# Gated products of a conv feed-forward and rotary steps, moved from GpSimd to VectorE

## The chip, the cores and the metric

The kernel runs on one core of a Trainium2 chip. The metric is the device time of one execution in microseconds (us); lower is better. Engine names are those of the profile: PE is TensorE (PEld its weight loads), DVE is VectorE, ACT is ScalarE, POOL is GpSimd, SP the engine that issues most transfers.

## What is computed

Two transformer-like blocks of two layers each, on 256 tokens of width 1024, in float32. A layer of the first block mixes tokens (a Fourier branch and a retention branch whose queries and keys are rotated), then runs a feed-forward with a convolution over three neighbouring tokens and a gate. A layer of the second block has pooling, a spatial gate and an attention whose latent queries and keys are rotated, then a squared-ReLU feed-forward. The parts that the change touches:

```python
def rotary(t):                    # block 1: queries and keys of the retention
    t1, t2 = t[..., :half], t[..., half:]
    return concatenate([t1 * cos - t2 * sin, t1 * sin + t2 * cos], axis=-1)

def conv_ffn(h, w_up, conv_w, conv_b, w_down):          # block 1
    u = h @ w_up                                        # 1024 -> 2 * 2816
    u = sum(pad(u)[:, i:i + S] * conv_w[i] for i in range(3)) + conv_b
    a, b = split(u, 2, axis=-1)
    return (gelu(a) * b) @ w_down

def apply_rope(x, cos, sin):                            # block 2
    x1, x2 = x[..., 0::2], x[..., 1::2]
    return stack([x1 * c - x2 * s, x1 * s + x2 * c], axis=-1)
```

## The kernel before

Activations lie feature-major, 128 features by 256 tokens to a tile (512 tokens in layer 0 of the second block, which carries a context beside the latent). Every product with weights is done in three matmuls: both sides are split into a rounded part and a remainder (hi and lo), and hi.hi, lo.hi and hi.lo are summed (`mm3`, lines 174 to 176).

Weights come as a stream of 540 units of 128x1024, eight 128x128 blocks each (`Stream`). For every unit SP loads `wraw`, ACT rounds it to `whi` (line 85) and DVE subtracts to get `wlo` (line 87); PE needs `wlo` for every third matmul. Beside that DVE works off modulation vectors, each a dot product over a 128x1024 tile (line 262, `mraw` or `junk`), paced by unit numbers (`RATES1`).

The feed-forward of block 1 runs over m = 0 to 21 in each of two layers. A step m takes two products with `ffn_up` (16 blocks, two units, 48 matmuls). Of each product ACT makes `z` (line 824) and DVE adds the two neighbouring tokens to it (lines 825 and 826). Then ACT makes `ga`, the Gelu of the first `z` (line 829); POOL multiplies it with the second `z` into `gb` (line 834); and `split` makes `fh` on ACT (line 179) and `fl` on DVE (line 180) of it, the input of `ffn_down`.

In block 1 `rotary` (lines 629 to 638) makes each of two halves with two products on DVE (`ra`, `rb`, lines 633 and 634), a sum or difference on POOL (`ro`, line 636) and a `split`: 16 sums in a layer. In block 2 `roped` (lines 1019 to 1026) makes a product and a shuffle on DVE (lines 1022 and 1023), a product and a sum on POOL (lines 1024 and 1025), and a split of the result: eight times in a layer, for keys and queries of four head pairs.

The order of instructions on each engine is set when the program is built: a scheduler places them, engine by engine, from what each depends on and its own estimates. Each engine then works through its list in that order, and an instruction that waits holds up all behind it.

Of the kernel before, what the change touches and what calls it, by code (L numbers as in the profile page):

```python
# [11 lines left out]
ALU = mybir.AluOpType  # L12
# [117 lines left out]
def build(ctx, tc, a, out):  # L130
    nc = tc.nc
# [20 lines left out]
    def tt(tag, name, shape, dt=F32):  # L152
        tag = cur["alias"].get(tag, tag)
        return cur["tp"].tile(list(shape), dt, name=name, tag=tag, bufs=cur["bufs"][tag])
# [23 lines left out]
    def split(src, hi, lo):  # L178
        nc.scalar.copy(hi, src)  # L179
        nc.vector.tensor_sub(lo, src, hi.bitcast(F32))  # L180
# [35 lines left out]
    def col(name, i, n=1):  # L216
        o = COLS[name] + i
        return cols[:, o:o + n]
# [85 lines left out]
    def fm(reqs, rhs, fresh=False, at=None):  # L304

        p = ps_mm.tile([128, 512], F32, name="mm")
        n = rhs[0][0].shape[-1]
        late = []
        for i, (r, (xh, xl)) in enumerate(zip(reqs, rhs)):
            wh, wl = st.take(*r) if isinstance(r[0], str) else r  # L310
            if at and i in at:
                at[i]()
            if fresh:
                nc.tensor.matmul(p[:, :n], wh, xh, start=(i == 0), stop=False)
                nc.tensor.matmul(p[:, :n], wl, xh, start=False, stop=False)
                late.append((wh, xl))
            else:
                mm3(p[:, :n], wh, wl, xh, xl, i == 0, i == len(reqs) - 1)
        for i, (wh, xl) in enumerate(late):
            nc.tensor.matmul(p[:, :n], wh, xl, start=False, stop=(i == len(late) - 1))  # L320
        return p[:, :n]
# [214 lines left out]
    with ExitStack() as c1:  # L536
# [78 lines left out]
        cos, sin = rope[:, 0, :], rope[:, 1, :]  # L615
# [4 lines left out]
        for l in range(2):  # L620
# [7 lines left out]
            def rotary(c0, dst, ps=None):  # L628
                p1, p2 = ps or (fm(win(c0), rhs), fm(win(c0 + 128), rhs))
                for j, (ca, cb, op) in enumerate(((cos, sin, ALU.subtract), (sin, cos, ALU.add))):  # L630
                    ta = tt("r", "ra", (128, 256))
                    tb = tt("r", "rb", (128, 256))
                    nc.vector.tensor_mul(ta, p1, ca)
                    nc.vector.tensor_mul(tb, p2, cb)
                    o = tt("ro", "ro", (128, 256))
                    nc.gpsimd.tensor_tensor(out=o, in0=ta, in1=tb, op=op)
                    hi, lo = dst(j)
                    split(o, hi, lo)

            if l:  # L640
                pace["rate"] = 0
                y.shift(need(0, l, 0)[:, 0, :])
                keys = y.run([win(2 * D), win(2 * D + 128)], dst)
                kv0 = tt("kv", "kv", (128, 4, 2, 256), F32R)
                rotary(None, lambda j: (kv0[:, 0, j, :], kv0[:, 1, j, :]), keys)
# [170 lines left out]
            for m in range(M1):  # L816
                pace["rate"] = RATES1[l][4] if m else 0
                z = []
                for ab in range(2):
                    i = ab * M1 + m  # L820
                    p = first.pop(0) if first else fm(up(i), rhs2, fresh=m == 1)
                    w = lambda t: col("conv_w", (l * 3 + t) * 44 + i)
                    zz = tt("r", "z", (128, 256))
                    nc.scalar.activation(zz, p, AF.Identity, scale=w(1), bias=col("conv_b", l * 44 + i))
                    nc.vector.scalar_tensor_tensor(out=zz[:, 1:], in0=p[:, :-1], scalar=w(0), in1=zz[:, 1:], op0=ALU.mult, op1=ALU.add)  # L825
                    nc.vector.scalar_tensor_tensor(out=zz[:, :-1], in0=p[:, 1:], scalar=w(2), in1=zz[:, :-1], op0=ALU.mult, op1=ALU.add)  # L826
                    z.append(zz)
                ga = tt("ro", "ga", (128, 256))
                nc.scalar.activation(ga, z[0], AF.Gelu)
                if m % 8 == 0:  # L830
                    tg = ("kv", "A", "B")[m // 8]
                    fh, fl = tt(tg, "fh", S8, F32R), tt(tg, "fl", S8, F32R)
                o = tt("go", "gb", (128, 256))
                nc.gpsimd.tensor_tensor(out=o, in0=ga, in1=z[1], op=ALU.mult)  # L834
                split(o, fh[:, m % 8, :], fl[:, m % 8, :])
                hid.append((fh[:, m % 8, :], fl[:, m % 8, :]))
            g2 = need(0, l, 5)[:, 0, :]
# [31 lines left out]
    for l in range(2):  # L869
        with ExitStack() as c2:  # L870
# [16 lines left out]
            cos, sin = rope[:, 0, :], rope[:, 1, :]  # L887
# [54 lines left out]
            def gate(i, m):  # L942
                pg = fm(gate_w(l, i, m), rhs)
                th = tt("gt", "gt", (128, N))
                nc.scalar.activation(th, pg, AF.Tanh, scale=0.5)
                return th
# [15 lines left out]
            for j in range(2):  # L962
# [12 lines left out]
                for hf, s in ((0, s2), (1, s4)):  # L975
                    r = slice(64 * hf, 64 * hf + 64)
                    nc.vector.tensor_tensor(out=pd[r], in0=s[r, :, 8:264],
                                            in1=icnt[r, j, :].unsqueeze(1).broadcast_to((64, nseg, 256)), op=ALU.mult)
# [39 lines left out]
            def roped(p):  # L1018
                t1 = tt("r", "ra", (128, 256))
                t2 = tt("r", "rb", (128, 256))  # L1020
                o = tt("ro", "ro", (128, 256))
                nc.vector.tensor_mul(t1, p, cos)
                nc.vector.stream_shuffle(t2, p, swap)
                nc.gpsimd.tensor_tensor(out=t2, in0=t2, in1=sin, op=ALU.mult)  # L1024
                nc.gpsimd.tensor_tensor(out=o, in0=t1, in1=t2, op=ALU.add)
                return o

            def scaled_split(src, hi, lo):
# [152 lines left out]
            for m in range(KT):  # L1181
                t0, t1 = (early.pop(0) if early else gate(i, m) for i in range(2))
                branch("w_pool_out_2", m, por, t0, at(acc, m))
                o = tt("go", "go", (128, N))
# [5 lines left out]
            for m in range(KT):  # L1190
                th = gate(2, m)
                o = tt("go", "go", (128, N))
# [123 lines left out]
            if not both:  # L1316
                bc = to_rows(rsqrt_cols(sq_sums(tiles(x))))
                for k in range(KT):
                    o = tt("nu" if k < 5 else "r", "fin", (128, T))
# [95 lines left out]
def make(inputs):  # L1415
    import concourse.bacc as bacc

    arrays, A = _layout(inputs)
    nc = bacc.Bacc("TRN2", target_bir_lowering=False, num_devices=1, dynamic_dma_scratch_size=1024)
    aps = {k: nc.dram_tensor("in_" + k, v.shape, mybir.dt.from_np(v.dtype), kind="ExternalInput").ap() for k, v in arrays.items()}  # L1420
    aps["ws"] = nc.dram_tensor("in_ws", (N_UNITS, 128, 1024), F32, kind="ExternalInput").ap()
    out = nc.dram_tensor("out", (KT, 128, T), F32, kind="ExternalOutput").ap()
    with tile.TileContext(nc) as tc, ExitStack() as ctx:
        req = build(ctx, tc, aps, out)
    ins = {"in_" + k: v for k, v in arrays.items()}
    ins["in_ws"] = _pack(req, A)
    return nc, ins
# [11 lines left out]
```

## Time and profile before

| | us |
|---|---|
| median of three runs | 2169.05 (2163.69 to 2169.51) |
| the profiled execution's own time | 2171.02 |
| its span, first to last instruction | 2169.2 |
| PE busy | 2089.8 |
| DVE busy | 1681.2 |
| ACT busy | 1008.6 |
| POOL busy | 291.5 |

Busy time is the time in which an engine has at least one instruction under way; instructions of one engine overlap by some tens of nanoseconds, so that the sum of their lengths is more. Matmuls of PE overlap much more: one of 256 columns has a length of some 0.28 us, and the next starts long before it ends. What lies between span and own time is outside of the first and last instruction.

### The profile page before, as it was taken

To read this page: it belongs to the slowest core of one execution; us is meant where nothing else is said; L and a number is where in the kernel's file an instruction comes from. 1 tells how busy PE (TensorE), PEld (TensorE's weight loads), DVE (VectorE), ACT (ScalarE), POOL (GpSimd) and SP (SyncE) were. 2 spreads that over 40 slices of the span, in tenths; PEclk is the share of its full clock that TensorE was granted. 3 is DMA by queue.
4 is the path that set the end of the run, shared out by engine and by line. 5 is a ranking of instruction groups with operands and counts; after the bars stand their busy time and mean duration, and the time that the engine had idled before them with its cause. 6 is when DMAs were issued, how large, how long until landed. Compare 5 with 4: busy or idle time off the path is not lost.

```text
span 2169.2 us, 36942 instructions
## 1 busy us (share of the span) xinstructions
PE 2089.8 (96%) x14492; PEld 1923.8 (89%) x14492; DVE 1681.2 (78%) x2849; ACT 1008.6 (46%) x1670; POOL 291.5 (13%) x342
## 2 busy tenths in 40 slices
PE   7999999999999999999999999999999989999998
PEld 6999999999999998898778888888888887899998
DVE  3778888887789888897878677788787577768665
ACT  3544466545445565554553233523233454556444
POOL 0002022222012022241110001200001112101000
PEclk9999999999999999999999999999999999999999
DMA  7576756685777655663334444355554243355553
GB/s 287 190 241 218 259 189 214 223 313 193 240 272 248 219 183 196 216 223 128 110 121 146 170 162 144 117 184 177 184 183 146 88 156 97 127 185 166 185 185 118
DMA packets 112350, 401.32 MB, mean 185 GB/s; under 512 B 12592, under 2 KB 14512, under 8 KB 110896
## 3 DMA queue, kind: packets, MB, share of 16 engines
q1 hardware_dynamic: 106272, 387.82, 52.4%
q10 hardware_dynamic: 5904, 11.14, 1.6%
q8 instruction: 114, 1.87, 0.4%
q14 instruction: 60, 0.49, 0.1%
HBM read 397.87 MB, written 1.05 MB: 184 GB/s over the span
## 4 chain that ended last, share of the span: by engine, by line
PE 80%; DVE 9%; POOL 4%; issue 3%; ACT 3%; DMA 1%; POOLq 0%; ACTq 0%; SPq 0%; DVEq 0%
PE mm L175 21%; PE mm L176 21%; PE mm L174 21%; DVE wlo L87 3%; PE mm L349 2%; PE mm L344 2%; PE mm L348 2%; POOL gb L834 2%; ACT whi L85 1%; DVE z L825 1%; DVE z L826 1%; PE sc L1055 1%; PE at L1095 1%; DVE mraw L262 1%; POOL rb L1024 1%
## 5 line engine op out<-in xcount | busy, mean ns | idle before, releaser
L85 ACT CAST whi<-wraw 128x1024 fp32r<-128x1024 f32 x540 | 564.5, 1047 | 701.2 <-PE mm L175 507.9
L87 DVE TENSOR_TENSOR wlo<-wraw,whi 128x1024 fp32r<-128x1024 f32 x540 | 667.6, 1238 | 169.0 <-ACT whi L85 166.2
L176 PE MATMUL mm<-hh,wlo 128*128 128x256 f32 (+1 forms) x2112 | 659.7, 313 | 12.1 <-DVE wlo L87 12.0
L174 PE MATMUL mm<-hh,whi 128*128 128x256 f32 (+1 forms) x2112 | 660.6, 313 | 3.4 <-ACT whi L85 2.4
L175 PE MATMUL mm<-hl,whi 128*128 128x256 f32 (+1 forms) x2112 | 657.8, 311 | 0.0
L176 PEld LDWEIGHTS mm<-hh,wlo 128*128 128x128 f32 x2112 | 401.6, 190 | 38.7 <-DVE wlo L87 15.1
L174 PEld LDWEIGHTS mm<-hh,whi 128*128 128x128 f32 x2112 | 402.0, 190 | 28.7 <-ACT whi L85 3.2
L175 PEld LDWEIGHTS mm<-hl,whi 128*128 128x128 f32 x2112 | 401.9, 190 | 22.9
L176 PE MATMUL mm<-fh,wlo 128*128 128x256 f32 (+1 forms) x880 | 275.4, 313 | 3.5 <-DVE wlo L87 3.4
L174 PE MATMUL mm<-fh,whi 128*128 128x256 f32 (+1 forms) x880 | 275.4, 313 | 1.6 <-ACT fh L179 1.6
L262 DVE CUSTOM_DVE_ANT_0 mraw<-mraw,cvec,cols 128x1024 f32<-128x1024 f32 x176 | 229.5, 1304 | 0.0
L176 PEld LDWEIGHTS mm<-fh,wlo 128*128 128x128 f32 x880 | 166.3, 189 | 14.8 <-DVE wlo L87 4.3
L174 PEld LDWEIGHTS mm<-fh,whi 128*128 128x128 f32 x880 | 166.3, 189 | 12.8 <-ACT fh L179 2.0
L175 PE MATMUL mm<-fh,whi 128*128 128x256 f32 (+1 forms) x528 | 176.2, 334 | 0.0
L349 PE MATMUL mm<-wlo,hh 128*128 128x256 f32 x496 | 140.5, 284 | 3.1 <-DVE wlo L87 3.1
L344 PE MATMUL mm<-whi,hh 128*128 128x256 f32 x496 | 141.2, 286 | 0.9 <-ACT hh L441 0.9
L348 PE MATMUL mm<-whi,hl 128*128 128x256 f32 x480 | 136.3, 284 | 0.0
L395 POOL TENSOR_TENSOR acc<-acc,sq 128x256 f32<-128x256 f32 x52 | 57.1, 1101 | 511.3 <-ACT sq L393 495.2
L262 DVE CUSTOM_DVE_ANT_0 junk<-mraw,cvec,cols 128x1024 f32<-128x1024 f32 x96 | 124.7, 1299 | 0.0
L175 PEld LDWEIGHTS mm<-fh,whi 128*128 128x128 f32 x528 | 99.7, 189 | 11.5 <-DVE fh L180 0.8
L175 PE MATMUL mm<-fl,whi 128*128 128x256 f32 x352 | 99.3, 282 | 0.1
L349 PEld LDWEIGHTS mm<-wlo,hh 128*128 128x128 f32 x496 | 94.6, 191 | 3.8 <-DVE wlo L87 3.3
(320 smaller groups left out, 3590.3 us busy)
## 6 DMA issues: line engine op xcount, KB each, us to landing
wraw<-in_ws SPq DMA_DIRECT2D x540, 512.0 KB, 3.3
mraw<-in_mw SPq DMA_DIRECT2D x176, 512.0 KB, 4.3
mraw<-in_mw SPq DMA_DIRECT2D x8, 1024.0 KB, 9.0
bias<-in_na_bias ACTq DMA_DIRECT2D x16, 256.0 KB, 2.8
dm<-in_dmask ACTq DMA_DIRECT2D x8, 256.0 KB, 3.9
cvec<-in_cvec SPq DMA_DIRECT2D x3, 512.0 KB, 5.3
x<-in_x SPq DMA_DIRECT2D x1, 1024.0 KB, 5.0
cx<-in_ctx ACTq DMA_DIRECT2D x1, 1024.0 KB, 7.6
```

The source lines that it names most:

```text
L85: self.nc.scalar.copy(hi, raw)
L87: self.nc.vector.tensor_sub(lo, raw, hi.bitcast(F32))
L174: nc.tensor.matmul(o, lh, rh, start=start, stop=False)
L175: nc.tensor.matmul(o, lh, rl, start=False, stop=False)
L176: nc.tensor.matmul(o, ll, rh, start=False, stop=stop)
L262: nc.vector.tensor_tensor_reduce(out=junk if b and not v else raw, in0=raw, in1=cvec[2 * b if v else b], scale=1.0, scalar=col("b_mod_2" i ...
L344: nc.tensor.matmul(o, xh, wh, start=(k == 0 and j % 2 == 0), stop=False)
L348: nc.tensor.matmul(o, xl, wh, start=False, stop=False)
L349: nc.tensor.matmul(o, xh, wl, start=False, stop=last and not fresh)
L395: (nc.gpsimd if k in SQ_POOL else nc.vector).tensor_tensor(out=acc, in0=acc, in1=sq, op=ALU.add)
L825: nc.vector.scalar_tensor_tensor(out=zz[:, 1:], in0=p[:, :-1], scalar=w(0), in1=zz[:, 1:], op0=ALU.mult, op1=ALU.add)
L834: nc.gpsimd.tensor_tensor(out=o, in0=ga, in1=z[1], op=ALU.mult)
```

## The change

Four instructions of the source move from `nc.gpsimd` to `nc.vector`, with the same operands: `gb`, the `ro` of block 1, and both steps of `roped`. In numbers that is 44 + 32 + 16 + 16 = 108 instructions of 128x256. Loads, tiles and buffers stay.

```diff
--- before.py
+++ after.py
@@ -633,7 +633,7 @@
                     nc.vector.tensor_mul(ta, p1, ca)
                     nc.vector.tensor_mul(tb, p2, cb)
                     o = tt("ro", "ro", (128, 256))
-                    nc.gpsimd.tensor_tensor(out=o, in0=ta, in1=tb, op=op)
+                    nc.vector.tensor_tensor(out=o, in0=ta, in1=tb, op=op)
                     hi, lo = dst(j)
                     split(o, hi, lo)
 
@@ -831,7 +831,7 @@
                     tg = ("kv", "A", "B")[m // 8]
                     fh, fl = tt(tg, "fh", S8, F32R), tt(tg, "fl", S8, F32R)
                 o = tt("go", "gb", (128, 256))
-                nc.gpsimd.tensor_tensor(out=o, in0=ga, in1=z[1], op=ALU.mult)
+                nc.vector.tensor_mul(o, ga, z[1])
                 split(o, fh[:, m % 8, :], fl[:, m % 8, :])
                 hid.append((fh[:, m % 8, :], fl[:, m % 8, :]))
             g2 = need(0, l, 5)[:, 0, :]
@@ -1021,8 +1021,8 @@
                 o = tt("ro", "ro", (128, 256))
                 nc.vector.tensor_mul(t1, p, cos)
                 nc.vector.stream_shuffle(t2, p, swap)
-                nc.gpsimd.tensor_tensor(out=t2, in0=t2, in1=sin, op=ALU.mult)
-                nc.gpsimd.tensor_tensor(out=o, in0=t1, in1=t2, op=ALU.add)
+                nc.vector.tensor_mul(t2, t2, sin)
+                nc.vector.tensor_add(o, t1, t2)
                 return o
 
             def scaled_split(src, hi, lo):
```

The scheduler places the moved instructions among DVE's others, and shifts others with them. Two places show it.

DVE, layer 1 of the feed-forward, around the split of one step (before; numbers in the names tell tiles apart, `mod101` is a modulation vector):

```order
L826 SCALAR_TENSOR_TENSOR z_10343<-mm_10310,cols_108,z_10343 128x255
L262 ISA mraw_10317,mod101_122<-mraw_10317,cvec_9204,cols_108 128x1024
L262 ISA mod101_122 128x1
L180 TENSOR_TENSOR fl_9913<-gb_10349,fh_9912 128x256
L825 SCALAR_TENSOR_TENSOR z_10385<-mm_10353,cols_108,z_10385 128x255
L87 TENSOR_TENSOR wlo_10435<-wraw_10432,whi_10434 128x1024
L826 SCALAR_TENSOR_TENSOR z_10385<-mm_10353,cols_108,z_10385 128x255
L825 SCALAR_TENSOR_TENSOR z_10421<-mm_10389,cols_108,z_10421 128x255
L87 TENSOR_TENSOR wlo_10470<-wraw_10467,whi_10469 128x1024
L826 SCALAR_TENSOR_TENSOR z_10421<-mm_10389,cols_108,z_10421 128x255
L87 TENSOR_TENSOR wlo_10513<-wraw_10510,whi_10512 128x1024
L180 TENSOR_TENSOR fl_9913<-gb_10427,fh_9912 128x256
```

The same place with the change:

```order
L826 SCALAR_TENSOR_TENSOR z_10343<-mm_10310,cols_108,z_10343 128x255
L87 TENSOR_TENSOR wlo_10393<-wraw_10390,whi_10392 128x1024
L834 TENSOR_TENSOR gb_10349<-ga_10347,z_10343 128x256
L825 SCALAR_TENSOR_TENSOR z_10385<-mm_10353,cols_108,z_10385 128x255
L262 ISA mraw_10317,mod101_122<-mraw_10317,cvec_9204,cols_108 128x1024
L262 ISA mod101_122 128x1
L180 TENSOR_TENSOR fl_9913<-gb_10349,fh_9912 128x256
L826 SCALAR_TENSOR_TENSOR z_10385<-mm_10353,cols_108,z_10385 128x255
L825 SCALAR_TENSOR_TENSOR z_10421<-mm_10389,cols_108,z_10421 128x255
L87 TENSOR_TENSOR wlo_10435<-wraw_10432,whi_10434 128x1024
L826 SCALAR_TENSOR_TENSOR z_10421<-mm_10389,cols_108,z_10421 128x255
L87 TENSOR_TENSOR wlo_10470<-wraw_10467,whi_10469 128x1024
```

Before, only `mraw` stood between the second pass over `z` and `fl`; now `wlo`, `gb`, the next step's first pass (line 825) and `mraw` stand there, with `gb` behind `wlo`.

DVE, block 2 layer 0, latent queries of head pair 1 (before; `P` of the attention is transposed and split into `pt`):

```order
L1022 TENSOR_TENSOR ra<-mm,rope_12374 128x256
L1023 STREAM_SHUFFLE rb<-mm 128x256
L87 TENSOR_TENSOR wlo<-wraw,whi 128x1024
L1030 SCALAR_TENSOR_TENSOR qq<-ro,qq 128x256
L1030 SCALAR_TENSOR_TENSOR qq<-mm,qq 128x256
L180 TENSOR_TENSOR pt<-at,pt 128x4x128 x2
```

The same place with the change:

```order
L1022 TENSOR_TENSOR ra<-mm,rope_12374 128x256
L1023 STREAM_SHUFFLE rb<-mm 128x256
L87 TENSOR_TENSOR wlo<-wraw,whi 128x1024
L1024 TENSOR_TENSOR rb<-rb,rope_12374 128x256
L1030 SCALAR_TENSOR_TENSOR qq<-mm,qq 128x256
L1025 TENSOR_TENSOR ro<-ra,rb 128x256
L180 TENSOR_TENSOR pt<-at,pt 128x4x128
L1030 SCALAR_TENSOR_TENSOR qq<-ro,qq 128x256
L180 TENSOR_TENSOR pt<-at,pt 128x4x128
```

Both steps of `roped` stand behind `wlo`, and the first half of `pt` now stands ahead of the rotated queries' remainder `qq<-ro`, which came before both halves.

## Rows read from the trace of the kernel before

**Rows 1.** The page: totals of the span, and chain that ended last, by engine.

```profile
PE 2089.8 (96%) x14492; PEld 1923.8 (89%) x14492; DVE 1681.2 (78%) x2849; ACT 1008.6 (46%) x1670; POOL 291.5 (13%) x342
...
PE 80%; DVE 9%; POOL 4%; issue 3%; ACT 3%; DMA 1%; POOLq 0%; ACTq 0%; SPq 0%; DVEq 0%
```

**Rows 2.** Windows: length, busy us (instructions) of PE, PEld, DVE, ACT, POOL; clock; DMA.

```profile
795.00:910.00 115.00, 107.15 (x884) 105.35 (x883) 96.06 (x161) 66.02 (x109) 27.46 (x18) 1.00 0.64 211
354.80:440.50 85.70, 83.47 (x693) 82.54 (x692) 69.72 (x111) 50.32 (x84) 21.92 (x15) 1.00 0.64 221
540.00:690.00 150.00, 149.65 (x1258) 149.24 (x1256) 129.03 (x213) 70.56 (x107) 22.50 (x28) 1.00 0.72 246
...
1040.00:1130.00 90.00, 84.39 (x437) 65.73 (x436) 74.26 (x204) 46.62 (x109) 17.80 (x16) 0.96 0.33 112
1090.00:1100.00 10.00, 7.88 (x49) 6.53 (x49) 6.66 (x18) 4.30 (x12) 2.50 (x2) 0.87 0.29 97
```

**Rows 3.** Timeline of POOL, `gb` of both layers, with idle time before each.

```profile
354.80 1.68 POOL L834 TENSOR_TENSOR gb<-ga,z 128x256 f32<-128x256 f32 x1 [4.03 <-DVE z L826]
...
440.48 1.55 POOL L834 TENSOR_TENSOR gb<-ga,z 128x256 f32<-128x256 f32 x1 [5.11 <-DVE z L826]
...
795.86 0.74 POOL L834 TENSOR_TENSOR gb<-ga,z 128x256 f32<-128x256 f32 x1 [6.57 <-DVE z L826]
...
912.09 1.66 POOL L834 TENSOR_TENSOR gb<-ga,z 128x256 f32<-128x256 f32 x1 [4.97 <-DVE z L826]
```

**Rows 4.** Timeline of one step of layer 1: start, length, engine, idle before.

```profile
846.45 0.48 DVE L826 SCALAR_TENSOR_TENSOR z<-mm,cols,z 128x255 f32<-128x255 f32 x1
...
847.10 1.61 POOL L834 TENSOR_TENSOR gb<-ga,z 128x256 f32<-128x256 f32 x1 [5.11 <-DVE z L826]
...
848.75 0.41 ACT L179 CAST fh<-gb 128x256 fp32r<-128x256 f32 x1 [1.82 <-POOL gb L834]
...
849.19 0.43 DVE L180 TENSOR_TENSOR fl<-gb,fh 128x256 fp32r<-128x256 f32 x1 [1.06 <-ACT fh L179]
849.53 0.48 DVE L825 SCALAR_TENSOR_TENSOR z<-mm,cols,z 128x255 f32<-128x255 f32 x1
...
855.65 0.43 DVE L180 TENSOR_TENSOR fl<-gb,fh 128x256 fp32r<-128x256 f32 x1 [1.07 <-ACT fh L179]
```

**Rows 5.** Waits of 795 to 910 us: who waited for whom, us, times, longest.

```profile
ACT fh L179 <- POOL gb L834: 36.1, 17, 3.0
DVE fl L180 <- ACT fh L179: 18.1, 17, 1.1
...
PE mm L176 <- DVE wlo L87: 7.5, 8, 1.5
```

**Rows 6.** POOL by line and form, whole span: busy us, mean ns, idle before.

```profile
L834 POOL TENSOR_TENSOR gb<-ga,z 128x256 f32<-128x256 f32 x44 | 62.7, 1424 | 204.3 <-DVE z L826 183.8 <-ACT whi L85 10.9 <-ACT z L824 5.5
...
L636 POOL TENSOR_TENSOR ro<-ra,rb 128x256 f32<-128x256 f32 x32 | 32.8, 1041 | 226.8 <-DVE rb L634 180.6 <-ACT whi L85 46.3
```

**Rows 7.** DVE by line and form, whole span, columns as before.

```profile
L180 DVE TENSOR_TENSOR ql<-ro,qh 128x256 fp32r<-128x256 f32 x16 | 10.1, 628 | 1.7 <-ACT qh L179 1.5
...
L796 DVE TENSOR_TENSOR go<-go,gf 128x256 f32<-128x256 f32 x16 | 6.8, 423 | 0.4
```

**Rows 8.** Timeline of the latent queries of head pair 1, block 2 layer 0.

```profile
1092.08 1.22 DVE L87 TENSOR_TENSOR wlo<-wraw,whi 128x1024 fp32r<-128x1024 f32 x1
...
1093.97 0.73 POOL L1025 TENSOR_TENSOR ro<-ra,rb 128x256 f32<-128x256 f32 x1
...
1095.19 0.42 DVE L1030 SCALAR_TENSOR_TENSOR qq<-ro,qq 128x256 fp32r<-128x256 f32 x1 [1.89 <-ACT qq L1029]
...
1095.87 1.28 DVE L180 TENSOR_TENSOR pt<-at,pt 128x512 fp32r<-128x512 f32 x2
1096.60 3.08 PE L1095 MATMUL at<-pt,vv 128*128 128x256 f32 x16 [2.12 <-DVE pt L180]
1099.48 0.63 PE L174 MATMUL mm<-hh,whi 128*128 128x512 f32 x1
```

## The prediction

> **What bounds the kernel now.** The page's totals come first: PE is busy 96% of the span and DVE 78%, POOL only 13% [rows 1]. PE is the engine to fill, and what can be won is the time in which it lacks work. Its busy share hides a part of that, since matmul lengths overlap, so I count matmuls per time instead. In a stretch in which PE is busy 149.65 of 150 us, 1258 matmuls, nearly all of 256 columns, take 150 us: 0.119 us each [rows 2]. A step of the feed-forward, 48 matmuls, therefore needs 48 x 0.119 = 5.72 us of PE.
>
> The page's chain then says where to look: POOL has 4% of what ended last, though it is nearly idle [rows 1]. The starts of `gb`, one to a step, give the real pace of the feed-forward. In layer 1, 18 steps take 912.09 - 795.86 = 116.2 us, 6.46 us each; in layer 0, 14 steps take 440.48 - 354.80 = 85.7 us, 6.12 us each [rows 3]. Against 5.72 us PE loses 0.74 us a step in layer 1 and 0.40 us in layer 0.
>
> The windows over these steps tell who sets that pace. In layer 1 DVE is busy 96.06 of 115 us and PE's matmuls thin out; ACT has 66.02, POOL 27.46 [rows 2]. DVE is thus busy 96.06 / 115 x 6.46 = 5.39 us a step and idle for 1.07. The waits say what it is idle for: of its some 19 idle us, 18.1 lie ahead of `fl`, which waits for `fh` on ACT, and ACT waits 36.1 us for `gb` on POOL; PE in turn waits for `wlo`, DVE's work [rows 5]. One step of the timeline shows the loop: DVE ends `z`, POOL takes 1.61 us for `gb`, ACT starts `fh` at 848.75, and DVE, idle for 1.06 us, starts `fl` at 849.19; the next `fl` is at 855.65 and has waited 1.07 us [rows 4]. So DVE is the bound of layer 1, and a sixth of its time there is a wait for POOL. In layer 0 it is busy 69.72 of 85.7 us [rows 2], 4.98 us a step.
>
> **The change, part by part.**
>
> *Gated products.* 44 instructions of 1424 ns leave POOL [rows 6]. On DVE the same kind, two inputs in SBUF and 128x256, takes 423 ns [rows 7]; what it adds to the list may be less, for the instruction behind `fl` started 849.53 - 849.19 = 0.34 us after it though `fl` is 0.43 long [rows 4]. I take 0.42. `gb` no longer waits for another engine but for `ga`, which ACT finishes earlier, and DVE always has a `wlo`, a dot product or a pass over `z` between `gb` and `fl`, so that ACT's 0.41 us for `fh` [rows 4] is covered. The 1.07 us of waiting is replaced by 0.42 us of work. Behind the wait stood the next `wlo`, and behind that PE.
>
> Layer 1: a step then costs DVE 5.39 + 0.42 = 5.81 us, a little over PE's 5.72. If no idle time is left, 18 steps gain 18 x (6.46 - 5.81) = 11.7 us. I keep 0.09 us a step for waits that turn up next, the likeliest being the first pass over `z`, which waits for ACT and through it for PE: **-10 us**. The best end, with 0.34 for `gb`, is 18 x (6.46 - 5.73) = 13; the worst, all idle time kept and the work on top, is 18 x 0.42 = 7.6 us lost.
>
> Layer 0: DVE would need 4.98 + 0.42 = 5.40 us, less than PE's 5.72, so PE becomes the bound and 14 x 0.40 = 5.6 us are to be had. The dot products come at some steps and not at others, and where one comes DVE is over 5.72 for that step; I take **-4.5 us**. The ends are -5.6 and 14 x 0.42 = +5.9.
>
> *Rotary of block 1.* 32 sums of 1041 ns leave POOL [rows 6] and bring DVE 32 x 0.42 = 13.4 us. In the stretch from 540 to 690 us, in which layer 1 rotates heads, PE is busy 149.65 of 150 and DVE is idle for 21 of 150 [rows 2]: nothing to win, and room for the 5 us that fall there. **0 us.** What hides it is that idle time and the units loaded ahead; without this cover the price is at most the 13.4. DVE also gets something back: `ql`, the remainder after these sums, takes 628 ns where its shape takes 423 [rows 7], 16 x 0.2 = 3.3 us. I count neither and keep -1 and +2 as ends.
>
> *Rotary of block 2.* Two instructions for each of eight results in a layer move, 16 x 0.35 = 5.6 us of DVE a layer at the spacing seen above. DVE is busy 74.26 of 90 us in the first of the two attentions, and PE only 84.39 of 90 [rows 2]. The one clear place is the latent queries of head pair 1: POOL's second step starts at 1093.97, `qq<-ro` on DVE starts at 1095.19 after 1.89 us of idle time, `pt` is behind it, and PE stands 2.12 us until `pt`; its matmuls of 512 columns are then 0.63 us long and the granted clock of these 10 us is 0.87, so a part runs at 1.2 GHz and not at 2.4 [rows 8, 2]. In the new order `wlo` (1092.08 to 1093.30) is still followed by three instructions of some 0.35 us and then the first half of `pt`, which starts near 1094.4 rather than 1095.87: 1.5 us for PE, and I add 0.5 for the clock: **-2 us**. At the other places `wlo` or a softmax step now stands ahead of the rotation, and I expect no net effect. Ends: -5, most of the 5.6 us that PE is not busy in that stretch, and +5.6, all of one layer's added work on the path.
>
> *Queues.* No transfer moves but one modulation load, which changes places with a weight load on SP: nothing.
>
> *Sum.* -10 - 4.5 + 0 - 2 = -16.5 us. The profiled execution, 2171.0 us with what lies around its span, becomes 2154.5. It stands 2.0 us above the median of the runs, so I forecast 2169.05 - 16.5 = **2152.5 us**.
>
> So DVE gains by taking work on, though at 84% of the stretch it is the most occupied of DVE, ACT and POOL [rows 2]: its idle sixth is made by the slow engine. The Trainium skill (Perfetto Trace Analysis, Optimizing Scalar/DVE Operations) says that work may be worth moving off a saturated DVE, even to GpSimd, though the port that the two share may spoil it; by this rule the change goes the wrong way, and the time would be that of the second rival.
>
> **The rivals.**
>
> *The wait only changes its name.* `fh` stands in ACT's list between `whi` and `z`, each of which can wait for PE. If ACT comes to `fh` late in every step, DVE keeps half of its idle time: 0.53 left + 0.42 new against 1.06 is a gain of 0.11 us a step, 32 steps, some 3.5 us: 2165.5. For it: ACT is busy 66.02 of 115 us with an order of its own. Against: ACT itself sat idle 36.1 us for `gb` [rows 5], so it has been early, not late.
>
> *DVE is simply too full.* Nothing of the idle time goes, because `fl` waits for something other than POOL, and DVE's list is 0.42 us longer in each step: 18 x 0.42 + 14 x 0.42 = 13.4 us, 2182.5. It decides from 6.46 - 5.81 = 0.65 us of idle time left per step in layer 1 on; below that the change still gains. For it: DVE's own sum, 5.81, is above PE's 5.72. Against: the wait is seen to follow POOL's end, 848.71 to 848.75 to 849.19, in step after step [rows 4, 5].
>
> That the change does less than it says is ruled out by the order of DVE's list, in which the moved instructions stand.
>
> **How the numbers follow.** Forecast 0.77, its own range 2145.5 (-13 - 5.6 - 5) to 2162.5 (a third of the idle time left in both layers, nothing in attention); first rival 0.14; second rival 0.09. The range that leaves out no more than 2 in 10 is 2146 to 2165: the forecast and the near side of the first rival. About 0.3%, 6.5 us, is what a measurement of this kernel can tell from no change, so faster means below 2162.5 and slower above 2175.6. Faster: 0.77 from the forecast, and 0.02 of the first rival, less 0.01 at the forecast's edge: 0.78. Same: the rest of the first rival and 0.01 of the others, 0.14. Slower: 0.08 of the second rival.
>
> **What would show it.** In layer 1 of the feed-forward `gb` starts should be 5.8 us apart, in layer 0 5.7; the wait of `fl` for `fh` should be gone; DVE should be busy some 97% of the steps of layer 1, and PE's wait for `wlo` there, 7.5 us [rows 5], a fraction. POOL's share of the chain should fall to about 1%. PE should stay full from 540 to 690 us. If `fl` still waits half a microsecond in each step, the first rival is right; if `gb` starts are over 6.5 us apart in layer 1, the second; if the feed-forward gains 14 us and the total does not, the attention or the rotation of block 1 has taken it.

## The result and the profile after

The changed kernel takes 2133.86 us (median of four runs, 2132.19 to 2134.51), the kernel before 2168.99 us in the same comparison: a ratio of 0.9839, 95% interval 0.9827 to 0.9851. The gain is 35 us, twice the 16.5 that was forecast, and the time lies below the range given. The profiled execution took 2132.19 us, its span 2130.4.

The page after, totals and chain, answers to [rows 1]:

```profile
PE 2077.2 (97%) x14492; PEld 1916.9 (90%) x14492; DVE 1696.6 (80%) x2957; ACT 1013.5 (48%) x1670; POOL 158.8 (7%) x234
...
PE 89%; DVE 5%; ACT 2%; issue 1%; POOL 1%; DMA 1%; ACTq 0%; POOLq 0%; SPq 0%; DVEq 0%
```

DVE has 108 instructions more and only 15.4 us more of busy time. POOL's share of the chain falls from 4% to 1%, DVE's from 9% to 5%, and PE's rises from 80% to 89%.

Windows of the changed kernel over the stretches of [rows 2] (length, then busy us and instructions of PE, PEld, DVE, ACT, POOL; granted clock; DMA): layer 1 and layer 0 of the feed-forward, the head rotations of block 1, and the attentions of block 2, layer 0 and layer 1.

```profile
790.00:905.00 115.00, 115.00 (x964) 114.55 (x962) 112.46 (x191) 73.40 (x117) 0.00 (x0) 1.00 0.70 236
348.00:434.00 86.00, 86.00 (x725) 86.00 (x724) 79.86 (x133) 54.50 (x89) 0.00 (x0) 1.00 0.70 234
530.00:680.00 150.00, 149.87 (x1260) 149.54 (x1259) 130.15 (x230) 71.45 (x106) 6.38 (x14) 1.00 0.73 250
...
1010.00:1130.00 120.00, 119.55 (x636) 94.25 (x635) 108.39 (x286) 62.89 (x139) 0.55 (x1) 1.00 0.37 128
1750.00:1850.00 100.00, 99.61 (x713) 89.47 (x713) 82.36 (x214) 53.06 (x102) 3.91 (x12) 1.00 0.36 118
```

In layer 1 of the feed-forward PE is busy all of the 115 us, with 964 matmuls where there were 884, and DVE 112.46 us. In both attentions PE is busy over 99%. The next rows show three short pieces of the attentions in the kernel before, and below them the two attentions in full; [rows 2] has a window over the first alone:

```profile
1049.70:1053.10 3.40, 3.40 (x10) 2.72 (x9) 2.66 (x10) 0.78 (x1) 0.00 (x0) 0.50 0.00 0
1097.50:1100.90 3.40, 3.40 (x15) 3.11 (x14) 2.48 (x11) 2.31 (x9) 0.00 (x0) 0.50 0.00 0
1797.20:1804.00 6.80, 6.26 (x17) 4.55 (x18) 3.44 (x13) 1.86 (x5) 0.04 (x1) 0.50 0.19 70
1030.00:1150.00 120.00, 114.24 (x593) 89.78 (x592) 99.39 (x254) 59.15 (x131) 18.35 (x17) 0.97 0.35 119
1780.00:1880.00 100.00, 91.98 (x629) 80.75 (x629) 74.29 (x189) 47.49 (x93) 21.03 (x28) 0.97 0.33 106
```

The second attention lost more than the first, 8 us of PE against 5.8, and three pieces, 13.6 us together, ran at a granted clock of 0.50, that is 1.2 GHz and not 2.4. In the changed kernel the clock is 1.00 throughout both.

The starts of `gb`, now on DVE, first and last of layer 0 and of layer 1, answer to [rows 3]:

```profile
352.26 0.42 DVE L834 TENSOR_TENSOR gb<-ga,z 128x256 f32<-128x256 f32 x1
...
432.69 0.43 DVE L834 TENSOR_TENSOR gb<-ga,z 128x256 f32<-128x256 f32 x1
...
784.87 0.42 DVE L834 TENSOR_TENSOR gb<-ga,z 128x256 f32<-128x256 f32 x1
...
889.17 0.41 DVE L834 TENSOR_TENSOR gb<-ga,z 128x256 f32<-128x256 f32 x1
```

14 steps of layer 0 take 80.43 us, 5.75 each, and 18 of layer 1 104.30 us, 5.79 each. The waits from 790 to 905 us answer to [rows 5] (waiter, releaser, us in all, times, longest):

```profile
ACT fh L179 <- DVE gb L834: 13.0, 15, 1.3
...
DVE fl L180 <- ACT fh L179: 0.5, 1, 0.5
```

DVE's wait ahead of `fl` is gone, 18.1 us to 0.5; ACT's ahead of `fh` is 13.0 where it was 36.1, and PE's matmuls wait for no `wlo` there (one weight load does, 0.2 us).

**Where the time went.** Both kernels run the same 14492 matmuls, but not all in the same order: the scheduler moved matmuls within PE's list too, at a few places of the feed-forward and at many in the two attentions. At the ends of the stretches below the same matmuls lie behind in every run, so there the k-th can be matched with the k-th. The table is worked out from the starts of matched matmuls: the time, in us, that each profiled execution needs less than the profiled one of before in a stretch between two matmuls (times of the trace before). What lies ahead of 69 us is left out: the profiled run of before began 1.0 to 3.5 us slower than all others, whatever their change. Names of the runs are explained in the next section. Between 69 and 312 us no run differs, but for 3.7 us of the last.

```
stretch of before   312-565   565-757  757-943  943-1029  1029-1330  1330-1762  1762-1980
what it holds       FFN 0     heads    FFN 1    context   attn 0     FFN        attn 1
the change            6.1       0.5     13.2     -3.1       8.2        1.2       10.0
gb alone              6.4       0.0     13.4     -3.1      -0.3        1.0        1.3
block 2 alone        -0.7       0.1     -1.2     -0.1       7.4        1.4       10.0
block 1 alone         1.3       0.5     -0.1      0.0      -0.4        1.0       -0.2
late split            6.3       0.0      7.4     -0.1      -0.5        1.2       -0.2
half of block 2      -0.7       0.0     -1.2     -0.1       7.2        0.7        8.0
block 2, late split   3.6       0.0      7.0     -0.1       8.2        1.6       10.0
gb twice              6.5       0.2      6.9     -1.2       7.7       -2.2       10.3
one place back        8.7       0.5     12.9     -3.1       8.1        1.2        7.8
all on DVE           10.2       0.4     14.5      0.0       7.4       -2.1        9.9
```

Stretches in which two runs do the same still differ by up to 2.6 us (the first column, the change and one place back), so smaller numbers say little by themselves.

The feed-forward gave 6.1 + 13.2 - 3.1 = 16.2 us, close to what was forecast. Of the rest, 18 us came from the two attentions, where 2 had been forecast.

### The profile page after: what moved, and what is told of

It is laid out like the page before. It is cut to its first block, busy times and chain, and to the rows that moved or that the text cites. A ratio compares the mean times of both kernels' runs of the same rounds, so it can differ in the third digit from the quotient of the medians.

```text
span 2130.4 us, 36855 instructions
## 1 busy us (share of the span) xinstructions
PE 2077.2 (97%) x14492; PEld 1916.9 (90%) x14492; DVE 1696.6 (80%) x2957; ACT 1013.5 (48%) x1670; POOL 158.8 (7%) x234
## 4 chain that ended last, share of the span: by engine, by line
PE 89%; DVE 5%; ACT 2%; issue 1%; POOL 1%; DMA 1%; ACTq 0%; POOLq 0%; SPq 0%; DVEq 0%
PE mm L176 24%; PE mm L175 24%; PE mm L174 24%; PE mm L349 3%; PE mm L344 3%; PE mm L348 3%; DVE wlo L87 2%; PE sc L1055 1%; ACT whi L85 1%; DVE nu L440 1%; PE at L1095 1%; PE at L1084 1%; PE mm L320 1%; PE mm L315 0%; PE mm L314 0%
## 5 line engine op out<-in xcount | busy, mean ns | idle before, releaser
L176 PEld LDWEIGHTS mm<-fh,wlo 128*128 128x128 f32 x880 | 167.0, 190 | 13.2 <-DVE wlo L87 2.7
L344 PEld LDWEIGHTS mm<-whi,hh 128*128 128x128 f32 x496 | 94.0, 189 | 1.8 <-ACT hh L441 1.7
```

The costliest lines, as they stand in the source:

```text
L176: nc.tensor.matmul(o, ll, rh, start=False, stop=stop)
L344: nc.tensor.matmul(o, xh, wh, start=(k == 0 and j % 2 == 0), stop=False)
```

## Experiments

### Each part alone

Three kernels make one part of the change each, from the kernel before. The gated products:

```diff
-                nc.gpsimd.tensor_tensor(out=o, in0=ga, in1=z[1], op=ALU.mult)
+                nc.vector.tensor_mul(o, ga, z[1])
```

> Only the gated products move; both rotary steps stay on GpSimd. Theory A (the parts are separate, and each gains the waits that it removes): matmul for matmul the traces of before and of the change part by 3.2 us in layer 0 of the conv feed-forward and 13.0 us in layer 1, so some 16 us less, about 2153 us, with steps of 5.7 us in layer 1 and the attention of block 2 as before. Theory B (what was won comes from a GpSimd that no longer shares anything with VectorE, in proportion to its work taken off): 62.7 of the 131 us of GpSimd's moved work, so 35 x 0.48 = 17 us here too, which this run cannot tell from A; the next three do.

Measured: 2152.95 us against 2168.53, ratio 0.9926 (0.9911 to 0.9940): -15.6 us.

The two rotary steps of block 2:

```diff
-                nc.gpsimd.tensor_tensor(out=t2, in0=t2, in1=sin, op=ALU.mult)
-                nc.gpsimd.tensor_tensor(out=o, in0=t1, in1=t2, op=ALU.add)
+                nc.vector.tensor_mul(t2, t2, sin)
+                nc.vector.tensor_add(o, t1, t2)
```

> Only the two rotary steps of block 2 move. Theory A: the traces part by 8.2 us in the first attention of block 2 and 10 us in the second, so 18 us less, about 2151 us; no granted clock under 0.95 in any 10 us of the two attentions, where before shows 0.80 to 0.87. Theory B: 36 of 131 us of moved work, 35 x 0.27 = 9.6 us, 2159. The sum on record had 2 us for this part, 2167.

Measured: 2151.57 us, ratio 0.9917 (0.9902 to 0.9932): -17.0 us.

The sum of block 1:

```diff
-                    nc.gpsimd.tensor_tensor(out=o, in0=ta, in1=tb, op=op)
+                    nc.vector.tensor_tensor(out=o, in0=ta, in1=tb, op=op)
```

> Only the rotary sums of block 1 move. Theory A: TensorE never lacked work while heads are rotated, so nothing there; but the traces also part by 3.5 us before 70 us and by 2.9 us where layer 1 starts with the rotation of its first keys, so 3 to 6 us less if both belong to this part, 0 if neither does: 2163 to 2169. Theory B: 33 of 131 us, 35 x 0.25 = 8.8 us, 2160.

Measured: 2167.97 us, ratio 1.0002 (0.9992 to 1.0011): no difference.

The parts add up: -15.6 - 17.0 - 0.6 = -33 us against -35. Theory B, a gain in proportion to the work taken off POOL, is out: it has 17, 9.6 and 8.8 us. Most of the miss, 15 of 18.6 us, lies in the rotary steps of block 2. The place that cost most is the first head pair's queries of layer 1. Timeline of the kernel before there (start, length, engine, line, idle time before and its releaser):

```profile
1790.40 0.74 POOL L1024 TENSOR_TENSOR rb<-rb,rope 128x256 f32<-128x256 f32 x1 [14.59 <-ACT whi L85]
...
1790.41 1.81 DVE L87 TENSOR_TENSOR wlo<-wraw,whi 128x1024 fp32r<-128x1024 f32 x1
...
1791.22 1.60 POOL L1025 TENSOR_TENSOR ro<-ra,rb 128x256 f32<-128x256 f32 x1
...
1792.86 0.41 ACT L179 CAST kk<-ro 128x256 fp32r<-128x256 f32 x1 [2.08 <-POOL ro L1025]
...
1793.30 0.42 DVE L180 TENSOR_TENSOR kk<-ro,kk 128x256 fp32r<-128x256 f32 x1 [1.08 <-ACT kk L179]
...
1794.04 0.40 PE L176 MATMUL mm<-hh,wlo 128*128 128x512 f32 x1
...
1794.83 1.61 POOL L1024 TENSOR_TENSOR rb<-rb,rope 128x256 f32<-128x256 f32 x1 [2.01 <-DVE rb L1023]
1796.52 0.72 POOL L1025 TENSOR_TENSOR ro<-ra,rb 128x256 f32<-128x256 f32 x1
1797.28 0.42 ACT L1029 ACTIVATE qq<-ro 128x256 fp32r<-128x256 f32 x1 [3.06 <-POOL ro L1025]
...
1797.74 1.65 PE L1055 MATMUL sc<-kk,qq 64*128 64x512 f32 x6 [3.31 <-ACT qq L1029]
```

It is the same loop as in the feed-forward, twice in a row: POOL is late with the rotated keys, so ACT waits 2.08 and DVE 1.08 us, and DVE therefore comes late to the queries' product and shuffle. POOL then takes 2.4 us for the queries, and PE stands 3.31 us. After that PE's matmuls run at 1.2 GHz (the row of 1797.20 above). The same place in the changed kernel:

```profile
1760.99 1.23 DVE L87 TENSOR_TENSOR wlo<-wraw,whi 128x1024 fp32r<-128x1024 f32 x1
...
1764.62 0.39 PE L176 MATMUL mm<-hh,wlo 128*128 128x512 f32 x1
...
1765.45 0.42 DVE L1024 TENSOR_TENSOR rb<-rb,rope 128x256 f32<-128x256 f32 x1
...
1765.90 0.42 DVE L1025 TENSOR_TENSOR ro<-ra,rb 128x256 f32<-128x256 f32 x1
...
1766.36 0.42 ACT L1029 ACTIVATE qq<-ro 128x256 fp32r<-128x256 f32 x1 [2.12 <-DVE ro L1025]
...
1766.48 0.40 PE L175 MATMUL mm<-hl,whi 128*128 128x512 f32 x1
...
1766.83 0.97 PE L1055 MATMUL sc<-kk,qq 64*128 64x512 f32 x6
```

From the first product (line 1022 for the keys, 1789.52 before and 1760.10 after) to the scores' matmul (`sc`) it is 8.2 us before and 6.7 after, and PE doesn't wait at all.

Two things did that, not one. The matmul of 1794.04 and that of 1764.62 are the same. In the kernel before it is PE's last one ahead of the scores; in the changed kernel eight more matmuls of 512 columns, some 0.23 us each, stand between it and the scores. With PE's old order the scores would still have waited, by an estimate from these rows, some 1.9 us for the queries. The next table has this for the first head pair's queries of both layers: the time from that matmul's start to the end of `qq` on ACT, worked out from the traces, and how many matmuls the scheduler placed in between (the last two runs are explained below).

```
                    layer 0                  layer 1
                    us to qq   matmuls       us to qq   matmuls
before                2.28        0            3.65        0
the change            1.91        8            2.15        8
block 2 alone         1.90        8            2.15        8
half of block 2       2.13        6            3.14        7
one place back        1.91        8            2.47        1
```

So at these two places the queries come 0.4 and 1.5 us sooner, and eight matmuls, 1.9 us, fill the time until they come. No run has the rotary steps on DVE and PE's old order, so no run parts the two.

### Is it GpSimd's work or the wait for it?

The product stays on POOL, and its `split` is issued one step later, so that `fh` and `fl` stand further behind it in ACT's and DVE's lists.

```diff
+            late = []
...
-                split(o, fh[:, m % 8, :], fl[:, m % 8, :])
+                if late:
+                    split(*late.pop())
+                late.append((o, fh[:, m % 8, :], fl[:, m % 8, :]))
                 hid.append((fh[:, m % 8, :], fl[:, m % 8, :]))
+            split(*late.pop())
```

> The kernel before, with everything on GpSimd as it was, but the split of a gated product is issued one step of the feed-forward later, so that nothing in VectorE's or ScalarE's list waits for GpSimd's 1.4 us. Theory A (the wait was the price, not the engine): the feed-forward gains as in the run with gated products alone, 13 to 16 us less, about 2154, VectorE some 85% busy there. Theory B (GpSimd's work beside VectorE was the price): nothing, 2169.

Measured: 2155.04 us, ratio 0.9940 (0.9923 to 0.9956): -13.5 us, with POOL's products no shorter than before (1516 ns on the mean). Most of what the gated products cost was the place of the waiting instruction in the two lists. PE's matmuls stand in the same order here as in the kernel before, as far as their names tell, so the gain isn't one of PE's order. In layer 1 it gains less than the move, 7.4 us against 13.4; the window from 795 to 910 us, and then the waits in it, say why:

```profile
795.00:910.00 115.00, 110.46 (x913) 108.93 (x913) 101.72 (x167) 66.42 (x114) 30.24 (x20) 1.00 0.65 221
```

```profile
ACT fh L179 <- POOL gb L835: 45.3, 18, 2.8
DVE fl L180 <- ACT fh L179: 12.5, 18, 1.1
```

DVE still waits 12.5 us there, and PE's 913 matmuls are between the 884 of before and the 964 of the change; a step was not enough.

### Half of the rotation, and one place

The product of `roped` moves, the sum stays:

```diff
-                nc.gpsimd.tensor_tensor(out=t2, in0=t2, in1=sin, op=ALU.mult)
+                nc.vector.tensor_mul(t2, t2, sin)
                 nc.gpsimd.tensor_tensor(out=o, in0=t1, in1=t2, op=ALU.add)
```

> The kernel before with one of the two rotary instructions of block 2 on VectorE: the product by the sines (L1024); the sum (L1025) stays on GpSimd. Both moved alone gave -17.0 us. Theory A (what counts is how late the queries come at the few places where TensorE stands, up to 3.31 us of waiting there and the stretch at 1.2 GHz after it): the product is the longer part (1.61 against 0.42 us at 1794.8 us of the trace before), so most of the lateness goes, and with it the half-clock stretches: 2153 to 2160 us, ratio 0.993 to 0.996. Rival (every crossing to GpSimd costs a wait of its own, and the crossing is still there): at most a quarter of the gain, 2164 us or more, ratio 0.998 or more.

Measured: 2154.9 us against 2168.08, ratio 0.9941 (0.9926 to 0.9956): -13.2 us, within the first theory's range. With the crossing to POOL still there, three quarters of the gain come, so a crossing has no great price as such. But the gain doesn't show that the queries' lateness went, as that theory has it: at the first head pairs they come only 0.15 and 0.5 us sooner than before, and six and seven more matmuls stand ahead of the scores (the table above). There most of what PE no longer waits is PE's new order.

The changed kernel with POOL back at one place, the queries shown above:

```diff
-            def roped(p):
+            def roped(p, eng=nc.vector):
...
-                nc.vector.tensor_mul(t2, t2, sin)
-                nc.vector.tensor_add(o, t1, t2)
+                eng.tensor_tensor(out=t2, in0=t2, in1=sin, op=ALU.mult)
+                eng.tensor_tensor(out=o, in0=t1, in1=t2, op=ALU.add)
...
-                    scaled_split(roped(p[:, 0:256]), qq[:, 0, 0:256], qq[:, 1, 0:256])
+                    scaled_split(roped(p[:, 0:256], nc.gpsimd if l and j == 0 else nc.vector), qq[:, 0, 0:256], qq[:, 1, 0:256])
```

> The changed kernel with the two rotary instructions of one single place back on GpSimd: the first head pair's latent queries of layer 1 (2 of 36 instructions or so). It puts a price on one late place. Theory A (the wait costs itself, 3.31 us in the trace before, and the stretch at 1.2 GHz behind it, 6.83 us long there, costs half its length, 3.4 us): +5 to +7 us, 2139 to 2141 us, and the trace shows a granted clock of 0.5 within the attention of layer 1. Rival B (only the wait): +3 us, 2137 us, granted clock 1.00 there. Rival C (the place is filled by other matmuls once the rest runs on VectorE): 0, 2134 us.

Measured: 2131.31 us, ratio 0.9834 (0.9819 to 0.9848), not to be told from the changed kernel's 0.9839. By the medians alone the third theory holds. The trace of that kernel says otherwise, a timeline and a window of it:

```profile
1761.87 1.72 POOL L1024 TENSOR_TENSOR rb<-rb,rope 128x256 f32<-128x256 f32 x1 [17.67 <-ACT whi L85]
...
1762.43 0.39 PE L176 MATMUL mm<-hh,wlo 128*128 128x512 f32 x1
...
1764.48 0.42 ACT L1029 ACTIVATE qq<-ro 128x256 fp32r<-128x256 f32 x1 [2.43 <-POOL ro L1025]
...
1764.95 1.35 PE L1055 MATMUL sc<-kk,qq 64*128 64x512 f32 x6 [1.89 <-ACT qq L1029]
```

```profile
1764.90:1768.50 3.60, 3.55 (x11) 2.40 (x12) 2.15 (x9) 0.47 (x1) 0.00 (x0) 0.56 0.21 83
```

PE waits 1.89 us and then gets a mean clock of 0.56 for 3.6 us. Matched matmul by matmul this kernel falls 3.8 us behind the changed one at this place, and has 1.6 us of it back within the next 15 us. PE's order differs between the two there, so a part of both figures may come from matching unlike matmuls; what stays at the stretch's end is the 2.2 us of the table (10.0 to 7.8). That is less than the medians can tell here: single runs of one kernel differ by 2 to 4 us. So the size that was expected, 5 to 7 us, is wrong; wait and clock are both seen in the trace, and the median doesn't decide.

Nor is it a clean price of a late place. POOL's two instructions make the queries only 0.3 us later than in the changed kernel, 2.47 us after the matmul of 1762.43 against 2.15. The scheduler, though, puts one matmul between that one and the scores and not eight, and these seven, 1.6 us, are most of the 1.89. Of the 3.31 us of before, 1.2 (3.65 - 2.47) were the lateness that came with the keys on POOL.

### Has DVE room?

The gated product is made twice on DVE, the rest is as in the changed kernel:

```diff
                 nc.vector.tensor_mul(o, ga, z[1])
+                nc.vector.tensor_mul(o, ga, z[1])
```

> The changed kernel with every gated product of the conv feed-forward computed twice on VectorE (the same product into the same tile): 44 more instructions of 0.42 us, 18.4 us of VectorE work. It asks how much room VectorE has left. Theory A (VectorE is full in layer 1's steps, 112.46 of 115.00 us, and not in layer 0's, 50.10 of 54.00 us): the 20 steps of layer 1's window need 112.46 + 20 x 0.42 = 120.9 us, 5.9 more than the window, layer 0 gains next to nothing: 2133.9 + 6 = 2140 us, 2138 to 2146. Rival (TensorE sets the step and VectorE has slack that the busy share doesn't show): 2134 to 2136 us. A second rival (the wait of ScalarE behind the product, not VectorE's total, decides): each step 0.42 us later in both layers, 44 x 0.42 = 18 us, 2152 us.

Measured: 2140.75 us, ratio 0.9872 (0.9856 to 0.9889), some 7 us over the changed kernel, in the first theory's range. The window of 790 to 905 us:

```profile
790.00:905.00 115.00, 112.27 (x926) 110.66 (x926) 113.65 (x204) 70.01 (x116) 0.00 (x0) 1.00 0.65 222
```

In layer 1 PE loses 38 of 964 matmuls in 115 us, and the table has 6.9 instead of 13.2 us; layer 0 takes the 22 extra products for nothing (6.5 against 6.1). That is 6.3 us, as the first theory has it. The rest of the table doesn't belong to it and cancels in part: 1.9 us less are lost in the context's stretch, and 3.4 more ahead of layer 1's attention, where both kernels have the same instructions. So in layer 1 the changed kernel stands close to the point where DVE's list and PE's take the same time; beyond it DVE is too full, as the prediction's second rival had it.

### Two ways to do the same with less

The rotary steps of block 2 on DVE, `gb` on POOL with the late split (the edits of two runs above together):

> The kernel before with the rotary instructions of block 2 on VectorE, the gated products left on GpSimd, and the split of each product issued one step later, so that ScalarE and VectorE don't stand behind GpSimd. The parts alone gave -17.0 and -13.5 us. If they add, 2168.7 - 30.5 = 2138 us; VectorE has 18 us less work than in the changed kernel. Theory A (the waits were the price; VectorE's extra work in layer 1 costs a little): 2133 to 2140 us, as fast as the changed kernel within 6 us. Rival (GpSimd's products slow VectorE's splits while both run): 2145 us or more.

Measured: 2139.22 us, ratio 0.9867 (0.9852 to 0.9882): the two parts add (-17.0 - 13.5 = -30.5, measured -28.9), and it ends 5 us behind the changed kernel. The table puts all of it into the feed-forward, 3.6 + 7.0 us instead of 6.1 + 13.2 - 3.1, where the late split alone had left DVE 12.5 us of waits.

The changed kernel with the late split:

> The changed kernel with the split of each gated product issued one step later, as in the run that split late with the product on GpSimd. In the changed kernel ScalarE still waits 13.0 us for the product in layer 1 (15 times, 0.9 us each), but TensorE waits for nothing there (115.00 of 115.00 us busy). Theory (the step is set by TensorE now, so a wait of ScalarE costs nothing): no difference, 2131 to 2136 us. Rival (ScalarE's wait delays the weights' high parts, 3.9 us of TensorE's waiting in all): up to 4 us faster, 2130 us.

Measured: 2133.92 us, ratio 0.9844 (0.9830 to 0.9857): no difference. The edit halves ACT's wait for `gb` in 115 us of layer 1, 13.0 to 6.0 us, and doesn't remove it; what it takes off is worth nothing, as it should be where PE sets the step.

### The rest of GpSimd's work

```diff
-LOW_POOL, SQ_POOL = (1, 3, 5, 7), (3, 4, 5, 6)
+LOW_POOL, SQ_POOL = (), ()
```

This moves the remaining sums of squares (line 395) and low parts of the normed activations (line 447) to DVE, and takes 40 instructions off ACT that only prepared the latter.

> The changed kernel with the rest of GpSimd's elementwise work on VectorE too: the sums of the squared columns and the low parts of the normed activations (some 92 instructions of 128x256). In the changed kernel TensorE waits for GpSimd's results of these kinds 2.2 us in all (sums 1.2, low parts 1.0), and VectorE would have 92 x 0.42 = 38 us more work, in the norm stretches. Theory (what counts is the wait that ends last, not which engine works): at best 2 us faster, 2132 us; VectorE's extra work queues ahead of the weights' low parts that TensorE takes next, so some of it is paid: 2130 to 2142 us. Rival (GpSimd is slow, so every move away from it gains): 10 us or more faster, 2124 us or less.

Measured: 2126.71 us (2125.39 to 2132.19), ratio 0.9816 (0.9803 to 0.9830): the fastest of all: 7.2 us less than the run above, the changed kernel's equal, in the same comparison, and the two intervals only touch. It was under the range that the theory gave and not as far as the rival's. Three windows over norms, first of the changed kernel, then of this one:

```profile
296.00:340.00 44.00, 40.04 (x296) 38.34 (x296) 36.90 (x69) 29.55 (x53) 5.04 (x5) 0.92 0.53 173
755.00:780.00 25.00, 23.05 (x173) 22.02 (x172) 21.85 (x46) 18.56 (x36) 3.19 (x4) 0.93 0.42 141
925.00:950.00 25.00, 22.19 (x171) 21.79 (x170) 25.00 (x37) 14.50 (x25) 12.37 (x10) 0.93 0.52 180
```

```profile
294.00:338.00 44.00, 41.23 (x339) 40.40 (x338) 41.99 (x83) 30.43 (x53) 1.41 (x3) 1.00 0.57 191
747.00:773.00 26.00, 24.18 (x197) 23.38 (x196) 23.76 (x51) 18.24 (x35) 0.71 (x1) 1.00 0.50 175
918.00:942.00 24.00, 22.62 (x191) 22.41 (x190) 23.56 (x44) 12.91 (x21) 0.00 (x0) 1.00 0.49 170
```

PE's matmuls come denser and the granted clock is 1.00 in all three, where it was 0.92 and 0.93. So more went than the 2.2 us of waits that name POOL as the releaser: time at 1.2 GHz is in no list of waits. Which of it comes from POOL's lateness, which from the 40 instructions that ACT no longer has, and which from PE's order, that differs here too, was not parted. Not all of it is gain. Ahead of layer 1's attention it loses 3.3 us against the changed kernel (the table's 1330 to 1762). PE's longest wait there is for a `wlo` that stands behind low parts (`hl`) in DVE's list, as the theory had said of DVE's extra work:

```profile
1708.55 1.67 DVE L449 SCALAR_TENSOR_TENSOR hl<-nu,mod,hh 128x256 fp32r<-128x256 f32 x4
...
1710.13 1.22 DVE L87 TENSOR_TENSOR wlo<-wraw,whi 128x1024 fp32r<-128x1024 f32 x1
...
1711.41 0.58 PE L176 MATMUL mm<-hh,wlo 128*128 128x256 f32 x1 [5.03 <-DVE wlo L87]
```

A second wait for a `wlo`, 2.69 us at 1721.82, stands behind DVE's wait for a table that is still being loaded, `icnt` (2.16 us, 0.77 in the changed kernel).

## Why the prediction was wrong in size and right in sign

**Layer 1 of the feed-forward, -10.** Right. A step takes 5.79 us where 5.81 was forecast without the waits that were added, and the wait of `fl` is gone. By matched matmuls the 18 steps that were priced gain 10.3 us, and the steps beside them bring the stretch to 13.2. Of these 3.1 are given back in the next stretch, for which the prediction had no term: PE comes sooner to DVE's context norm and dot products (25.00 of 25.00 us busy in the window from 925 us above), waits 2.5 us there for a `wlo` where it was 1.7, and the clock in that window is 0.93. That the net, 10.1, is again the forecast is luck. DVE needs 112.46 / 115 x 5.79 = 5.66 us a step, 0.15 less than the sum had it.

**Layer 0, -4.5.** Right: 5.75 us a step, PE full; by matched matmuls the feed-forward gains 4.9 us from 354.8 to 460 us, and the stretch, with norms at both ends, 6.1. The run with `gb` alone, -15.6 us, answers to the two terms' sum of -14.5.

**Rotary of block 1, 0.** Right: ratio 1.0002.

**Rotary of block 2, -2.** This is the step that failed. The run with this part alone gives -17.0 us. The prediction worked out one place in one layer, head pair 1 of layer 0, and said of all others "I expect no net effect", from DVE's order alone. At the one place it came out as said: the first half of `pt` starts 2.15 us after `wlo` where it was 3.79, 1.6 us sooner against the 1.5 forecast, and PE's 2.12 us there are 0.25. What the prediction put at nothing were PE's waits at the other places, the half clock behind two of them, and that the scheduler would move PE's matmuls as well as DVE's instructions. In the trace of before PE waits for the attention's queries, `P` and `pt` 5.5 us in layer 0 and 8.0 us in layer 1, as these two groups of PE's waits show, from 1030 and from 1780 us:

```profile
PE at L1095 <- DVE pt L180: 2.1, 1, 2.1
PE sc L1055 <- ACT qq L1029: 1.9, 1, 1.9
...
PE at L1084 <- DVE pt L180: 3.6, 2, 1.9
PE sc L1055 <- ACT qq L1029: 3.3, 1, 3.3
```

In the changed kernel the same waits are 0.2 and 0.4 us, 12.9 us less. For the five longest, 11.0 us together, the traces say how they went, measured from the same PE matmul in both kernels. What PE waited for comes 0.4 and 1.5 us sooner at the first head pairs' queries, where eight matmuls fill the rest, and 1.7, 1.3 and 2.3 us sooner at the other three (1096.60, 1836.10 and 1860.48 us), where PE's order moves by at most four. By that estimate about two thirds are lateness that went, as the prediction's mechanism has it, and about one third, 3.7 us, is work that PE was given in the meantime. The half-clock pieces from 1049.70 and 1797.20, 10.2 of the 13.6 us, follow the two places where it was given most. The 13.6 us at a granted clock of 0.50 cost up to half their length, 6.8 us. Together that is 19.7 us at most, and the matched matmuls gained 8.2 + 10.0 = 18.2. Even the best end, "-5, most of the 5.6 us that PE is not busy in that stretch", was that of one layer: the prediction has no row of the second attention, and that has 8 us of PE's idle time. The term should have been bounded by both windows, 5.8 + 8.0 us, and by half of the time at clock 0.50.

**What the list of signs said.** All of them held: `gb` 5.75 and 5.79 us apart, no wait ahead of `fl`, DVE 98% busy in layer 1, no matmul waiting for `wlo` there, POOL at 1% of the chain, PE full in the rotations of block 1. Only the last clause spoke of the attention, and as a place where a gain might be lost.

**The rivals.** That the wait would only change its name is out: DVE's idle time ahead of `fl` went from 18.1 to 0.5 us. That DVE is too full is out for this change, but only just: the run with the product made twice is past that point in layer 1. The rule of the Trainium skill that the prediction set against the change (Perfetto Trace Analysis, Optimizing Scalar/DVE Operations: work off a saturated DVE, even to GpSimd, though the shared port may spoil it) would have had the second rival's time. Here the moved work cost DVE 0.42 us where its wait had cost it 1.07, and DVE, at 84% busy, was held up by that wait and not saturated. The late split says the same from the other side: with the work left on POOL and its consumers one step later, 13.5 of 15.6 us come.

## What to carry to other kernels

Price a slow helper engine by the instructions that wait for it in the in-order lists of busy engines, and by what stands behind those, not by its own busy time. When such a loop is found in one place, look for it at every place where the same helper is called, in every layer, and add up PE's missing busy time and the time at half clock over windows that cover them all. Where a scheduler places the instructions, compare every engine's order before and after, PE's too: a wait can go because its operand comes sooner or because other work was put ahead of it, and the time alone doesn't tell which. Before taking work onto the engine that is nearly the bound, compare its list with PE's per step: here 5.66 against 5.72 us, and one more instruction of 0.42 us was too much.

## What had not been expected of the hardware

- The DVE instructions below are longer while POOL works beside them. `wlo` of 1790.41 took 1.81 us with two POOL instructions in its time, the same one 1.23 us without (both rows above). `ql` of block 1 took 628 ns on the mean in the kernel before [rows 7], and in the changed one:

```profile
L180 DVE TENSOR_TENSOR ql<-ro,qh 128x256 fp32r<-128x256 f32 x16 | 6.7, 416 | 0.4 <-ACT qh L179 0.3
```

  The Trainium skill says that a DVE instruction with two SBUF inputs contends with a GpSimd instruction that reads SBUF (SBUF — State Buffer, Who interferes with whom); both rows agree. That could be one reason why 108 more instructions, 45 us at 0.42, raised DVE's busy time by only 15.4; how much of the rest is overlap between neighbours was not measured.
- The piece at half clock behind one and the same wait has no fixed length. The attention of the run with `gb` alone is that of the kernel before, and PE waits the same 3.31 us for the queries of layer 1. The second half of the 6.8 us that follow, first in the kernel before and then in that run:

```profile
1800.60:1804.00 3.40, 3.40 (x9) 2.63 (x9) 1.84 (x7) 1.45 (x4) 0.00 (x0) 0.50 0.02 5
```

```profile
1781.10:1784.50 3.40, 3.40 (x18) 2.42 (x17) 1.92 (x8) 2.16 (x5) 0.00 (x0) 0.99 0.02 5
```

  9 matmuls at a clock of 0.50 against 18 at 0.99; the table has 1.3 us for this attention, though nothing in it was changed.
